# Low-part score matmuls over 64 or over 128 rows in a hybrid attention kernel

## Chip, cores and metric

The kernel runs on one NeuronCore of a Trainium2 chip, as one launch. The metric is the device time of that launch in microseconds (us), the median of the runs; a profile of one execution (its span, its instructions and their waits) stands beside it.

## What is computed

Two layers of a diffusion backbone over 512 latent tokens and 256 context tokens, model width 1024, in f32. Each layer is feed-forward (SwiGLU), token mixing, feed-forward, with modulated norms around. Layer 0 mixes with differential attention (4 heads of 2 components of width 64) and multi-head latent attention (MLA, 4 heads, width 128 without position and 64 with a rotary key that all heads share). Layer 1 mixes with a state-space scan and a neighbourhood attention (NA, 8 heads of width 64). The change touches the scores alone:

```
def diff_attend(q, k, v, lam):
    s = jnp.einsum('bqhcd,bkhcd->bhcqk', q, k).astype(jnp.float32) * (DIFF_HD ** -0.5)
    p = jax.nn.softmax(s, axis=-1)
    a = (p[:, :, 0] - lam * p[:, :, 1]).astype(v.dtype)
    return jnp.einsum('bhqk,bkhe->bqhe', a, v)
...
    k = jnp.concatenate([k_nope, k_rope], axis=-1)
...
        s_lat = jnp.einsum('bqhd,bjqmhd->bhqjm', q_r, k_win).astype(jnp.float32) * scale + bias
        s_ctx = jnp.einsum('bqhd,bkhd->bhqk', q_r, k_ctx).astype(jnp.float32) * scale
```

## The kernel before

TensorE multiplies in fp32r, a rounded form of f32. To keep precision, operands are split into a high part H (the rounded value) and a low part L (the rest), and a product is three matmuls: H·H, H·L and L·H (`mm3`, lines 211 to 215). The low parts come from ACT (a cast) and DVE (a subtraction).

Heads of width 64 fill only half of the 128 rows over which TensorE contracts. `stacked` (line 249) uses that. It makes two tiles S[0] and S[1] of 128 rows, one for each of the two heads or components in a 128-row projection. Of a query, S[e] has H in the head's own half and L in the other half; of a key, H in both halves. The other half is filled by a DMA that POOL issues (line 257). One matmul of a query's S with a key's S over 128 rows is thus H·H + L·H. What is left is the query's H with the key's L: the key's low parts of both heads lie in one tile L, a head in each half, and the second matmul runs over the 64 rows of its head. `score2` (line 260) issues both, chunk by chunk of keys, with a slice r of 64 rows in the second:

```
            for e, out in outs:
                mm(out[:, c0:c0 + n], q[0][e][:, qs], k[0][e][:, ks], start=True, stop=False)
            for e, out in outs:
                r = slice(64 * e, 64 * e + 64)
                mm(out[:, c0:c0 + n], q[0][e][r, qs], k[1][r, ks], start=False, stop=True)
```

Lines 265 and 268 are the two. A unit of differential attention (`diff`, line 1073: a head and 128 queries) calls `score2` once per component, each time for one component alone, with key chunks of 512 and 256 columns (the last two units of a head, for context queries, have the 256 alone). A unit of NA (`na_unit`, line 1668) calls it for both heads at once, with two chunks of 256. A unit of MLA (`mla`, line 1112) has for each chunk three matmuls without position (lines 213 to 215), the rotary one over 128 rows (1128), and the rotary key's low part over the 64 rows of the head's half (1129). The shared rotary key is projected into both halves, so its H and L tiles have 128 rows already.

After the scores DVE takes the maximum (line 984), ACT the exponential (987), DVE the reciprocal of the sum (989); TensorE transposes the probabilities (994) and multiplies by the values (1067). `pipeline` (line 297) steps several units in turn and fills in quanta of projections that later heads need (`pf`; in NA the output projection `po`), as much per step as `set_share` allows. The order on each engine is drawn up when the program is built.

Most tiles in SBUF come from one pool `u` of 41 buffers (`NU`). PSUM has two wide score buffers (`ps`), each for one set of scores, so that the next set can be written while the last is read.

Of the kernel before, what the change touches and what calls it, by code (L numbers as in the profile page):

```python
# [9 lines left out]
F32 = mybir.dt.float32  # L10
F32R = mybir.dt.float32r
# [65 lines left out]
class Hybrid:  # L77
# [49 lines left out]
    def wload(self, src):  # L127
# [4 lines left out]
        r = self.wraws.pop(0) if self.wraws else self.wraw(src)  # L132
        H, L = [t[:, :n] for t in self.whl()]
        nc.scalar.copy(H, r)  # L134
        nc.vector.tensor_tensor(L, r, H.bitcast(F32), ALU.subtract)  # L135
        return [(H, L)]

    def wpair(self, srcs):
        def load():
# [3 lines left out]
            for i, src in enumerate(srcs):  # L143
                nc.sync.dma_start(r[:, i * n:(i + 1) * n], src)
            H, L = [t[:, :m * n] for t in self.whl()]
            nc.scalar.copy(H, r[:, :m * n])
            nc.vector.tensor_tensor(L, r[:, :m * n], H.bitcast(F32), ALU.subtract)
            return [(H[:, i * n:(i + 1) * n], L[:, i * n:(i + 1) * n]) for i in range(m)]
        return load
# [97 lines left out]
        (nc.gpsimd if pool else nc.vector).tensor_tensor(L, src, H.bitcast(F32), ALU.subtract)  # L247

    def stacked(self, f, n, key, name):
        nc = self.nc  # L250
        S = [self.u(n, F32R, name + "S") for _ in range(2)]
        L = self.u(n, F32R, name + "L")
        for e in range(2):
            r, o = slice(64 * e, 64 * e + 64), slice(64 - 64 * e, 128 - 64 * e)
            nc.scalar.copy(S[e][r], f[r])
            nc.vector.tensor_tensor(L[r], f[r], S[e][r].bitcast(F32), ALU.subtract)
            nc.gpsimd.dma_start(S[e][o], (S[e] if key else L)[r])
        return S, L

    def score2(self, outs, q, k, qs, chunks):  # L260
        mm = self.nc.tensor.matmul
        for c0, ks in chunks:
            n = ks.stop - ks.start
            for e, out in outs:
                mm(out[:, c0:c0 + n], q[0][e][:, qs], k[0][e][:, ks], start=True, stop=False)  # L265
            for e, out in outs:
                r = slice(64 * e, 64 * e + 64)
                mm(out[:, c0:c0 + n], q[0][e][r, qs], k[1][r, ks], start=False, stop=True)  # L268

    def evac_split(self, src, H, L, scale=None):  # L270
        nc = self.nc
# [736 lines left out]
    def mixer_ab(self):  # L1008
        nc, a = self.nc, self.a
# [37 lines left out]
        def to_cat(o, gcol, idx):  # L1047
            H, L = self.u(T, F32R, "catH"), self.u(T, F32R, "catL")
            for (_, c0, n) in STREAMS:
                pt = self.pb("pt")  # L1050
                self.transposes(o[:, c0:c0 + n], n // P, pt)
                self.evac_split(pt[:, :n], H[:, c0:c0 + n], L[:, c0:c0 + n], gcol)
            cat[idx] = (H, L)

        def turned(p, n):
            at = self.u(n * P, name="at")
            for t0 in range(0, n, 4):
                m = min(4, n - t0)
                pt = self.pb("pt")
                self.transposes(p[:, t0 * P:], m, pt)  # L1060
                nc.scalar.copy(at[:, t0 * P:(t0 + m) * P], pt[:, :m * P])
            return at

        def pv(at, kts, v, hd):
            po = self.pb("po")
            for i, kt in enumerate(kts):
                nc.tensor.matmul(po[:, :P], at[:, i * P:(i + 1) * P], v[hd][:, kt],
                                 start=i == 0, stop=i == len(kts) - 1)
            return po[:, :P]
# [42 lines left out]
        def mla(hd, qt):  # L1112
            self.tick(self.rate)
            if qt == 0:
                ods[4 + hd] = self.u(T, name="om")
            o = ods[4 + hd]
            rows = slice(64 * (hd % 2), 64 * (hd % 2) + 64)
            qn, kn, qr, kr = lat["qn"][hd], lat["kn"][hd], lat["qr"][hd // 2], lat["kr"]
            kts = range(6) if qt < 4 else range(4, 6)
            n = len(kts)  # L1120
            off = kts[0] * P
            qs = slice(qt * P, (qt + 1) * P)
            sc = self.ps("sc")
            for (c0, w) in self.key_chunks(qt):
                out = sc[:, c0 - off:c0 - off + w]
                self.mm3(out, (qn[0][:, qs], qn[1][:, qs]), (kn[0][:, c0:c0 + w], kn[1][:, c0:c0 + w]), True, False)
                qe = qr[0][hd % 2]
                nc.tensor.matmul(out, qe[:, qs], kr[0][:, c0:c0 + w], start=False, stop=False)
                nc.tensor.matmul(out, qe[rows, qs], kr[1][rows, c0:c0 + w], start=False, stop=True)
            p, r, _ = self.softmax_parts(sc, n * P)  # L1130
            yield
            at = turned(p, n)
            yield
            po = pv(at, kts, lat["v"], hd)
            nc.vector.tensor_scalar(o[:, qs], po, r, None, ALU.mult)
            if qt == 5:
                yield
                to_cat(o, None, 4 + hd)
# [34 lines left out]
        for hd in range(4):  # L1173
            items.append(lambda hd=hd: self.fill_until(lambda: len(lat.get("kn", ())) > hd))
            for qt in range(6):
                items.append(mla(hd, qt))
# [783 lines left out]
```

## Time and profile before

| | |
|---|---|
| time, median of 3 runs | 2925.66 us (2924.67 to 2929.27) |
| the profiled execution: its time / its span | 2928.09 us / 2926.0 us |
| mean granted clock of TensorE | 0.988 |
| PE (matmul) busy | 2854.9 us, 98%, 16429 instructions |
| PEld (weight load) busy | 2620.2 us, 90% |
| DVE busy | 2118.0 us, 72% |
| ACT busy | 1179.9 us, 40% |
| POOL busy | 92.5 us, 3% |

PE is TensorE's matmul, PEld its weight load, which overlaps it. A matmul's record lasts from its start until its result is out, and matmuls are pipelined: how long one holds the engine is read from its start to the next one's start. In a row of the order of time, "128*128 128x512" is the array's rows and columns in use, then the operand's partitions and columns, and "x2" merges equal neighbours. In names, S is a stacked tile, L a low part, H a high part; `sc` are scores of layer 0, `nsc` of NA. A stretch's row gives each engine's busy time and count, then the granted clock and the DMA share.

### The profile page before, as it was taken

The numbers are of one execution on the slowest core, as the hardware profiler recorded it, in microseconds if no ns is written. First come the engines' busy times: TensorE is split into PE (matmuls) and PEld (weight loads), VectorE is DVE, ScalarE is ACT, GpSimd is POOL, SyncE is SP. The second block draws the span as 40 slices with busy tenths as digits, with TensorE's granted clock in tenths as the row PEclk, the third lists the DMA queues.
The fourth block names the chain that finished last, engine by engine and source line by source line (L and its number), as shares of the span: only waits on it lengthen the run. The fifth ranks groups of instructions, "written<-read, shape, count | busy, mean of one in ns | idle before, by whom it ended". The sixth has DMA issues, their size and how long they took to land. (4 is left out here: it accounts for less than half of the span.)

```text
span 2926.0 us, 41798 instructions
## 1 busy us (share of the span) xinstructions
PE 2854.9 (98%) x16429; PEld 2620.2 (90%) x16429; DVE 2118.0 (72%) x3708; ACT 1179.9 (40%) x2177; POOL 92.5 (3%) x133
## 2 busy tenths in 40 slices
PE   6999999999999999999999999999999999999998
PEld 4899999987778899999999999999889887788887
DVE  5988888787664698888879677866877967733324
ACT  4332233445554343323346332333565655432222
POOL 0000000000000000000000000000000000010100
PEclk8999999999999999999999999999999999999999
DMA  6433343242100233333323233322233334232231
GB/s 229 130 129 116 123 133 112 73 124 56 35 25 10 80 96 113 112 122 129 110 78 101 74 129 123 130 65 67 73 90 107 99 114 121 89 101 95 93 98 61
DMA packets 105989, 290.00 MB, mean 99 GB/s; under 512 B 12480, under 2 KB 25664, under 8 KB 105792
## 3 DMA queue, kind: packets, MB, share of 16 engines
q1 hardware_dynamic: 100896, 278.65, 29.6%
q0 software_dynamic: 2880, 6.56, 1.1%
q8 instruction: 129, 2.11, 0.3%
q10 hardware_dynamic: 2016, 2.12, 0.2%
q14 instruction: 68, 0.56, 0.1%
HBM read 274.89 MB, written 5.83 MB: 96 GB/s over the span
## 5 line engine op out<-in xcount | busy, mean ns | idle before, releaser
L214 PE MATMUL po<-gL,wH 128*128 128x384 f32 (+2 forms) x1271 | 431.5, 340 | 0.0
L215 PE MATMUL po<-gH,wL 128*128 128x384 f32 (+2 forms) x1271 | 428.0, 340 | 0.0
L213 PE MATMUL po<-gH,wH 128*128 128x384 f32 (+2 forms) x1271 | 424.6, 342 | 2.7 <-DVE x L684 1.4
L134 ACT CAST wH<-wraw 128x1024 fp32r<-128x1024 f32 (+2 forms) x173 | 163.9, 949 | 419.3 <-PE po L214 148.5
L748 PE MATMUL pgu<-N,wH 128*128 128x384 f32 x960 | 321.5, 340 | 3.0 <-ACT wH L155 1.6
L749 PE MATMUL pgu<-N,wH 128*128 128x384 f32 x960 | 324.2, 338 | 0.0
L750 PE MATMUL pgu<-N,wL 128*128 128x384 f32 x960 | 322.7, 337 | 0.4 <-DVE wL L156 0.4
L155 ACT CAST wH<-wraw 128x1024 fp32r<-128x1024 f32 x180 | 162.9, 908 | 394.5 <-issue 130.7
L684 DVE SCALAR_TENSOR_TENSOR x<-po,half,x 128x128 f32<-128x128 f32 (+3 forms) x459 | 208.7, 492 | 118.5 <-PE po L215 117.2
L135 DVE TENSOR_TENSOR wL<-wraw,wH 128x1024 fp32r<-128x1024 f32 (+2 forms) x173 | 190.5, 1102 | 125.3 <-ACT wH L134 119.9
L213 PEld LDWEIGHTS po<-gH,wH 128*128 128x128 f32 x1271 | 237.4, 188 | 13.2 <-DVE x L684 2.3
L214 PEld LDWEIGHTS po<-gL,wH 128*128 128x128 f32 x1271 | 239.0, 188 | 7.6
L748 PE MATMUL pgu<-b,wH 128*128 128x384 f32 x720 | 245.3, 341 | 0.3 <-DVE vz L775 0.2
L215 PEld LDWEIGHTS po<-gH,wL 128*128 128x128 f32 x1271 | 238.7, 188 | 6.8
L749 PE MATMUL pgu<-b,wH 128*128 128x384 f32 x720 | 243.1, 338 | 0.0
L750 PE MATMUL pgu<-b,wL 128*128 128x384 f32 x720 | 242.8, 337 | 0.0
L156 DVE TENSOR_TENSOR wL<-wraw,wH 128x1024 fp32r<-128x1024 f32 x180 | 187.7, 1046 | 35.0 <-ACT wH L155 34.7
L748 PEld LDWEIGHTS pgu<-N,wH 128*128 128x128 f32 x960 | 180.4, 188 | 9.4 <-DVE xw L779 2.7
L750 PEld LDWEIGHTS pgu<-N,wL 128*128 128x128 f32 x960 | 180.3, 188 | 0.8 <-DVE wL L156 0.8
L749 PEld LDWEIGHTS pgu<-N,wH 128*128 128x128 f32 x960 | 180.5, 188 | 0.0
L426 DVE SCALAR_TENSOR_TENSOR wraw<-wraw,cb 128x1024 f32<-128x1024 f32 x128 | 156.1, 1220 | 6.2 <-DMA wraw<-in_wmodT 6.1
L155 ACT CAST wH<-wsum 128x1024 fp32r<-128x1024 f32 x60 | 63.1, 1052 | 235.3 <-DVE wsum L162 175.2
(389 smaller groups left out, 6398.2 us busy)
## 6 DMA issues: line engine op xcount, KB each, us to landing
wraw<-in_win SPq DMA_DIRECT2D x176, 512.0 KB, 3.3
wraw<-in_wmodT SPq DMA_DIRECT2D x128, 512.0 KB, 3.4
wraw<-in_wout SPq DMA_DIRECT2D x96, 256.0 KB, 3.1
wraw<-in_wout SPq DMA_DIRECT2D x48, 192.0 KB, 2.5
wraw<-in_wxbc SPq DMA_DIRECT2D x16, 512.0 KB, 3.6
E<-csd SPq DMA_DIRECT2D x32, 256.0 KB, 4.8
wraw<-in_wout SPq DMA_DIRECT2D x16, 448.0 KB, 3.3
wmod<-in_wmodA SPq DMA_DIRECT2D x16, 384.0 KB, 7.2
```

The costliest lines, as they stand in the source:

```text
L134: nc.scalar.copy(H, r)
L135: nc.vector.tensor_tensor(L, r, H.bitcast(F32), ALU.subtract)
L155: nc.scalar.copy(H, src)
L156: nc.vector.tensor_tensor(L, src, H.bitcast(F32), ALU.subtract)
L213: mm(out, l[0], r[0], start=start, stop=False)
L214: mm(out, l[0], r[1], start=False, stop=False)
L215: return mm(out, l[1], r[0], start=False, stop=stop)
L426: nc.vector.scalar_tensor_tensor(junk, r, 1.0, self.cb[s], ALU.mult, ALU.mult, accum_out=acc[:, s:s + 1])
L684: self.nc.vector.scalar_tensor_tensor(xs, acc.at(P, c0, n), scal[:, d, s:s + 1], xs, ALU.mult, ALU.add)
L748: mm(bank, w[0][:, c], r[0], start=start and kk == 0, stop=False, skip_group_check=True)
L749: mm(bank, w[0][:, c], r[1], start=False, stop=False, skip_group_check=True)
L750: mm(bank, w[1][:, c], r[0], start=False, stop=kk == 3, skip_group_check=True)
```

## The change

`stacked` makes, for a key, two low-part tiles instead of one. Each has one head's low part in that head's half and zeros, written by a memset on POOL, in the other. `score2` runs the second matmul over all 128 rows: the query's L, which now stands against the other half, meets zeros. Its order is by head or component: first and second product of one, then of the other. In MLA the slice of rows goes; the low part of the query now meets the rotary key's low part, a small product that was left out before.

```
     def stacked(self, f, n, key, name):
+
         nc = self.nc
         S = [self.u(n, F32R, name + "S") for _ in range(2)]
-        L = self.u(n, F32R, name + "L")
+        Ls = [self.u(n, F32R, name + "L") for _ in range(2)] if key else [self.u(n, F32R, name + "L")] * 2
         for e in range(2):
             r, o = slice(64 * e, 64 * e + 64), slice(64 - 64 * e, 128 - 64 * e)
+            L = Ls[e]
+            if key:
+                nc.gpsimd.memset(L[o].bitcast(F32), 0.0)
             nc.scalar.copy(S[e][r], f[r])
             nc.vector.tensor_tensor(L[r], f[r], S[e][r].bitcast(F32), ALU.subtract)
             nc.gpsimd.dma_start(S[e][o], (S[e] if key else L)[r])
-        return S, L
+        return S, Ls
...
             for e, out in outs:
-                mm(out[:, c0:c0 + n], q[0][e][:, qs], k[0][e][:, ks], start=True, stop=False)
-            for e, out in outs:
-                r = slice(64 * e, 64 * e + 64)
-                mm(out[:, c0:c0 + n], q[0][e][r, qs], k[1][r, ks], start=False, stop=True)
+                for part in range(2):
+                    mm(out[:, c0:c0 + n], q[0][e][:, qs], k[part][e][:, ks], start=part == 0, stop=part == 1)
...
-            rows = slice(64 * (hd % 2), 64 * (hd % 2) + 64)
...
-                nc.tensor.matmul(out, qe[rows, qs], kr[1][rows, c0:c0 + w], start=False, stop=True)
+                nc.tensor.matmul(out, qe[:, qs], kr[1][:, c0:c0 + w], start=False, stop=True)
```

On TensorE, the first unit of head 2 in differential attention. In these rows a name's number tells one tile from another, and the size is that of the output. Before:

```order
L265 MATMUL sc_6767<-kS_6330,qS_6128 128x512
L268 MATMUL sc_6767<-kL_6332,qS_6128 128x512
L265 MATMUL sc_6767<-kS_6330,qS_6128 128x256
L268 MATMUL sc_6767<-kL_6332,qS_6128 128x256
L265 MATMUL sc_6779<-kS_6331,qS_6129 128x512
L268 MATMUL sc_6779<-kL_6332,qS_6129 128x512
L265 MATMUL sc_6779<-kS_6331,qS_6129 128x256
L268 MATMUL sc_6779<-kL_6332,qS_6129 128x256
```

and now:

```order
L270 MATMUL sc_6779<-kS_6336,qS_6134 128x512
L270 MATMUL sc_6779<-kL_6338,qS_6134 128x512
L270 MATMUL sc_6779<-kS_6336,qS_6134 128x256
L270 MATMUL sc_6779<-kL_6338,qS_6134 128x256
L270 MATMUL sc_6791<-kS_6337,qS_6135 128x512
L270 MATMUL sc_6791<-kL_6339,qS_6135 128x512
L270 MATMUL sc_6791<-kS_6337,qS_6135 128x256
L270 MATMUL sc_6791<-kL_6339,qS_6135 128x256
```

The place of each matmul is the same; the low parts of the two components are two tiles (kL_6338, kL_6339) where they were one.

On TensorE, the first unit of the second head pair in NA. Before:

```order
L265 MATMUL nsc_22875<-nS_22759,nS_22655 128x256
L265 MATMUL nsc_22875<-nS_22760,nS_22656 128x256
L268 MATMUL nsc_22875<-nL_22761,nS_22655 128x256
L268 MATMUL nsc_22875<-nL_22761,nS_22656 128x256
L265 MATMUL nsc_22875<-nS_22759,nS_22655 128x256
```

and now:

```order
L270 MATMUL nsc_22893<-nS_22774,nS_22670 128x256
L270 MATMUL nsc_22893<-nL_22776,nS_22670 128x256
L270 MATMUL nsc_22893<-nS_22775,nS_22671 128x256
L270 MATMUL nsc_22893<-nL_22777,nS_22671 128x256
L270 MATMUL nsc_22893<-nS_22774,nS_22670 128x256
```

The two low-part matmuls of a chunk, one per head, stood next to each other; now each follows its own head's first product.

On POOL, the stacking of head 2 (first the query's tiles, then the key's) and what follows it. Before:

```order
L257 DMA qS_6128<-qL_6130 64x768
L257 DMA qS_6129<-qL_6130 64x768
L257 DMA kS_6330<-kS_6330 64x768
L257 DMA kS_6331<-kS_6331 64x768
L1104 TENSOR_TENSOR r_6535<-v_6533,neghalf_91 128x6
```

and now:

```order
L261 DMA qS_6134<-qL_6136 64x768
L261 DMA qS_6135<-qL_6136 64x768
L258 MEMSET kL_6338 64x768
L258 MEMSET kL_6339 64x768
L261 DMA kS_6336<-kS_6336 64x768
L261 DMA kS_6337<-kS_6337 64x768
L1106 TENSOR_TENSOR r_6544<-v_6542,neghalf_91 128x6
```

Both memsets stand ahead of the two DMAs that fill the key's other halves.

## Rows read from the trace of the kernel before

**Rows 1.** Busy time by stretch: us from the start, length, engines, clock, DMA share, GB/s.

```profile
655.00:750.00 95.00, 94.91 (x502) 71.31 (x501) 74.31 (x151) 51.46 (x128) 5.64 (x10) 1.00 0.22 62
750.00:845.00 95.00, 91.41 (x509) 71.99 (x509) 64.95 (x141) 50.80 (x132) 7.66 (x6) 0.98 0.08 22
805.00:815.00 10.00, 8.52 (x44) 6.58 (x44) 6.24 (x12) 4.26 (x9) 1.63 (x1) 0.86 0.09 28
845.00:938.00 93.00, 93.00 (x598) 74.74 (x597) 43.81 (x98) 44.90 (x113) 2.43 (x3) 1.00 0.04 11
2400.00:2520.00 120.00, 115.58 (x801) 88.01 (x800) 91.57 (x166) 65.26 (x158) 7.59 (x13) 0.97 0.38 107
```

**Rows 2.** Lines 268 and 1129: count, duration in ns (min/median/max), first and last start, forms.

```profile
L268 PE MATMUL sc<-kL,qS x80: 379/384/626, 656.4 to 836.0; 64*128 64x256 f32 x48, 64*128 64x512 f32 x32
L268 PE MATMUL nsc<-nL,nS x64: 378/381/385, 2399.3 to 2509.4; 64*128 64x256 f32 x64
L1129 PE MATMUL sc<-krL,qrS x40: 378/385/500, 845.5 to 934.9; 64*128 64x256 f32 x24, 64*128 64x512 f32 x16
```

**Rows 3.** Order of time on PE, a component in diff: start us, us, instruction.

```profile
739.57 0.50 PE L265 MATMUL sc<-kS,qS 128*128 128x512 f32 x1
740.00 0.49 PE L268 MATMUL sc<-kL,qS 64*128 64x512 f32 x1
740.42 0.38 PE L265 MATMUL sc<-kS,qS 128*128 128x256 f32 x1
740.73 0.38 PE L268 MATMUL sc<-kL,qS 64*128 64x256 f32 x1
741.04 0.50 PE L213 MATMUL pf<-hH,wH 128*128 128x512 f32 x1
741.38 0.39 PE L214 MATMUL pf<-hL,wH 128*128 128x512 f32 x1
741.61 0.39 PE L215 MATMUL pf<-hH,wL 128*128 128x512 f32 x1
```

**Rows 4.** Order of time on PE, the end of a unit's scores in MLA.

```profile
895.03 0.28 PE L215 MATMUL sc<-knH,qnL 128*128 128x256 f32 x1
895.15 0.28 PE L1128 MATMUL sc<-krH,qrS 128*128 128x256 f32 x1
895.35 0.38 PE L1129 MATMUL sc<-krL,qrS 64*128 64x256 f32 x1
895.67 0.33 PE L994 MATMUL pt<-cst,p 128*128 128x128 f32 x1
```

**Rows 5.** Order of time on PE, a unit's scores in NA.

```profile
2434.38 0.40 PE L265 MATMUL nsc<-nS 128*128 128x256 f32 x2
2434.72 0.39 PE L268 MATMUL nsc<-nL,nS 64*128 64x256 f32 x2
2435.03 0.50 PE L265 MATMUL nsc<-nS 128*128 128x256 f32 x2
2435.47 0.38 PE L268 MATMUL nsc<-nL,nS 64*128 64x256 f32 x2
2435.78 0.44 PE L994 MATMUL npt<-cst,np 128*128 128x128 f32 x2
```

**Rows 6.** Line 365, a memset on POOL: count, ns, start, form.

```profile
L365 POOL MEMSET sc<- x1: 311/311/311, 0.8 to 0.8; 128x256 f32 x1
```

**Rows 7.** Line 257, POOL's issues of the key copies in layer 0.

```profile
L257 POOL DMA_DIRECT2D kS<-kS x8: 509/509/517, 620.5 to 736.8; - x8
```

**Rows 8.** Waits of PE, 2400 to 2520 us: us in total, times, longest.

```profile
PE nsc L265 <- DMA nS<-nS: 1.8, 3, 0.9
```

**Rows 9.** Waits of DVE for ACT, 655 to 750 us.

```profile
DVE wL L135 <- ACT wH L134: 1.8, 3, 0.9
DVE rsum L989 <- ACT p L987: 1.6, 3, 1.0
```

**Rows 10.** Waits of DVE for the exponential, 750 to 845 us.

```profile
DVE rsum L989 <- ACT p L987: 4.9, 5, 2.1
```

## Prediction

> **What bounds the kernel now.** I read the views in this order. First the stretches [rows 1], to see who is full where the change acts. The reader is to see that TensorE (PE) is busy throughout 655 to 938 us, the two attentions of the first mixer (diff to about 845, MLA after it), and 115.58 of 120 us in the neighbourhood attention (NA), at a granted clock of 1.00 or little less, which is its 2.4 GHz level. DVE is the next engine, with 74.31 of 95 us in the first half of diff, less later. So what changes PE's queue in these stretches changes the end. Then the counts [rows 2]: every low-part matmul of a score runs on 64 rows of the array, and there are 80 in diff, 40 in MLA, 64 in NA, all between matmuls over 128 rows. A duration there says little, since matmuls overlap: 379 to 385 ns at half the rows is no shorter than its neighbours. So third the order of time, where the distance from one start to the next is what a matmul holds PE [rows 3 to 5].
>
> **What a half-row matmul costs.** Undisturbed, 512 columns over 128 rows hold PE for 0.23 us (741.38 to 741.61 [rows 3]), 256 columns for 0.12 (895.03 to 895.15 [rows 4]). Around a half-row matmul three distances are longer. The full-row matmul before it: 895.15 to 895.35 is 0.20 instead of 0.12, so 0.08 on entry. The half-row one: 895.35 to 895.67 is 0.32 instead of 0.12, 740.00 to 740.42 is 0.42 instead of 0.23, so 0.20. And the first full-row matmul after it: 741.04 to 741.38 is 0.34 instead of 0.23, so 0.11.
> Diff: from 740.00 to 741.38 [rows 3] stand four matmuls (512, 256, 256, 512 columns), 1.38 us; undisturbed they would hold 0.23 + 0.12 + 0.12 + 0.23 = 0.70. That is 0.68 for two half-row matmuls with one entry among them; with the other entry 0.76, 0.38 each. Times 80: **30.4 us**.
> MLA: the 16 on 512 columns are followed by a score matmul as in diff, 16 x 0.38 = 6.1. The 24 on 256 columns close a unit, mostly with transposes behind: 895.15 to 895.67 is 0.52 for two that would hold 0.24, 0.28 each (what the first transpose pays is left out), 6.7. Together **12.8 us**.
> NA: the two heads' low-part matmuls use different halves of the rows, and there the row shows two in the time of one: "x2" spans 0.39 us [rows 5]. The unit from 2434.38 to 2435.78 takes 1.40 for eight matmuls of 256 columns; over full rows 8 x 0.12 = 0.96. So 0.44 per unit, times 16 units **7.0 us**, with the lost overlap already in it.
> Sum 50.2 us. The number of matmuls is the same, the columns too; the row count is no part of what a matmul holds PE (a full-row one holds 0.23 for 512 columns).
>
> The Trainium skill speaks against the change here: its page "TensorE: Matmul & The Clock Gate", Part 3, section "The mechanism", has matmuls in distinct row groups overlap in the array, the next tile starting some 4 ns after the first. NA's pairs agree with it (0.39 us for two). By that rule alone, with nothing paid for going in and out, the sum would be a loss: 32 pairs that become two matmuls in a row.
>
> **What is added.** Per key, two memsets on POOL of 64 x 768, 16 in all. The trace has one of 128 x 256, 311 ns [rows 6]; three times the columns bound one by 0.31 and 0.93, I take 0.7 (width counts, not rows), 11 us on POOL over the kernel, which is busy 5.64 and 7.66 us in the halves of diff [rows 1]. In diff they stand in POOL's queue ahead of the copies of the key halves, so a memset that waits for its buffer holds these. The cover is long: the last of the eight key copies issues at 736.8 [rows 7], when head 2's first unit has not begun [rows 3], and head 3 is scored six units later. Heads 0 and 1 are copied during the projections. I cost them at nothing; without that cover it is 1.4 us per head. In NA the cover is short: PE already waits three times for a key copy, 1.8 us in all [rows 8]. Each of the three can grow by what the unit just before saves, 0.44, so I take off 1.3; with both memsets in the way it would be 1.4 more per head pair, 5.6, which is for the range.
> One more of the 41 shared buffers is held per key; a wait for one falls on the memset, so its bounds are nothing and the memset's cover above. The key tiles' zero half needs no DMA and no ACT or DVE time. For MLA the rotary key's low part already fills 128 rows, so nothing is added there.
>
> **What is late next.** DVE. In 655 to 750 it is busy 74.31 us and waits 3.4 for ACT (exponentials, weight parts) [rows 9], which a faster PE does not shorten: 77.7. PE has 48 of the half-row matmuls there (14 units, of which ten use both key chunks), so it needs 95 - 48 x 0.38 = 76.8. DVE is the longer by **0.9 us**. In the second half it is 64.95 + 4.9 [rows 10] = 69.9 against 95 - 32 x 0.38 = 82.8, with room. Two queues that close will catch on each other. The row for 805 to 815 shows the size of one such catch: PE busy 8.52 of 10 and clock 0.86, so 1.5 us idle and 2.8 us at the 1.2 GHz level, which costs half of that, 1.4. I take one more of these, **2.9 us** (an estimate, one episode of that row). In MLA DVE has 43.81 of 93 us, so no loss.
> Gain: 50.2 - 1.3 - 0.9 - 2.9 = 45.1 us. Against the profiled execution (span 2926.0, its own time 2928.09) that is 2880.9 and 2883.0; that execution is 2.4 us over the median of the three runs, 2925.66, from which I get **2881 us** (2880.6).
>
> **The rivals.**
> DVE takes the place of the switches: if in diff 24 of the 48 reciprocals wait their longest 1.0 us for the exponential [rows 9] with nothing to do between, DVE needs 77.7 + 69.9 + 24 = 171.6 of 190 us and diff gains 18.4 instead of 30.4 less 3.8. With MLA's 12.8 and nothing kept in NA: 31 us, 2894.5. For: DVE is at 78% of the first half. Against: only three of the reciprocals wait there now, since other DVE work lies between.
> All of it arrives: no catch anywhere, and transposes after MLA units gain too (0.05 each at most, by rounding of the rows): 52, 2873.5.
> The long distances stay, because they belong to accumulating a second product and not to the row count: then NA loses the overlap, 32 x 0.12 = 3.8 us, 2929.5. The rule of the Trainium skill's page "TensorE: Matmul & The Clock Gate" that is told above would leave it so too. Against: L214 is also a second product on the stationary tile of the matmul before it, into the same accumulation, and it holds PE for 0.23 [rows 3]; L1128 adds to the accumulation of L215 and starts 0.12 behind it [rows 4]. What differs at L268 and L1129 is the 64 rows.
> Slower: each unit of diff starves PE long enough for the clock to fall, as at 805 to 815. At the lower level PE loses half of the time spent there. It decides from 100 us of the 190 at that level, which eats the 50.2; at 120 us the loss is 60 and the time 2935.5. Against: in the first half, where DVE is fullest, the clock is 1.00 throughout, and PE's order has no fewer fill-in matmuls than now.
>
> **How the numbers follow.** Forecast (gain 37 to 55, with everything or a catch more) 0.72; DVE-bound (20 to 37) 0.2; distances stay 0.05; slower 0.03. About 0.2% (5.9 us) is what a measurement of this kernel can tell from no change. The first two cases are faster, 0.92; the third lies within, 0.05; the last 0.03. The range leaves out the last two and the thin ends: low 2870, 55 saved, the sum with 10% for rounding; high 2897, 28 saved, the DVE rival with NA's bound of 5.6 partly in it.
>
> **What would show it.** Right: the two lines of the score matmuls and the last of MLA's five all read 128*128; start to start 0.23 and 0.12 there, no 0.42; a diff component 0.70 instead of 1.4; the stretch that was 655 to 938 some 40 us shorter, NA some 6; PE's clock still 1.00; DVE's waits for score matmuls shorter, DVE at 85 to 95% of the first half of diff. POOL has 16 memsets of 0.3 to 0.9 us, and nobody waits for them. Wrong: score matmuls over 128 rows still 0.3 or 0.4 apart (the switch was not the cost); PE waiting for exponentials or for the transposes' inputs in each unit (DVE or ACT took over); PE waiting for key copies over 2 us at a time (memsets held by buffers); a granted clock under 0.95 in diff.

## The result, and the profile after

The changed kernel took a median of 2886.94 us (2885.11 to 2888.39, 4 runs), the kernel before 2927.47 (2924.67 to 2934.94, 4 runs): a ratio of 0.985, 95% interval 0.9838 to 0.9863. That is 40.5 us faster; forecast were 2881 us and a gain of 45.1. The profiled execution took 2888.18 us, its span 2886.2.

The page of the changed kernel, its span and the busy time of each engine:

```profile
span 2886.2 us, 41850 instructions
PE 2804.7 (97%) x16429; PEld 2614.9 (91%) x16429; DVE 2114.9 (73%) x3708; ACT 1179.0 (41%) x2177; POOL 105.3 (4%) x149
```

PE does the same 16429 matmuls with 50 us less of busy time; POOL has 12.8 us more. The stretches that answer to [rows 1] (start and end in us, length, busy time and count of PE, PEld, DVE, ACT and POOL, granted clock, DMA share, GB/s) are diff in two halves, MLA, and most of NA:

```profile
659.00:740.00 81.00, 79.03 (x512) 69.54 (x512) 74.92 (x154) 51.40 (x130) 9.27 (x13) 1.00 0.26 72
740.00:821.00 81.00, 75.73 (x492) 66.48 (x492) 61.89 (x136) 48.83 (x130) 8.38 (x6) 1.00 0.09 25
821.00:900.00 79.00, 78.34 (x586) 72.91 (x585) 43.09 (x96) 43.96 (x111) 2.43 (x3) 1.00 0.05 13
2362.00:2477.00 115.00, 108.87 (x805) 87.72 (x804) 91.02 (x165) 65.88 (x160) 11.95 (x19) 0.97 0.40 114
```

The first row holds about as many matmuls and DVE instructions as the first row of before, in 81 us instead of 95. DVE is now busy 92% of it (85 to 95 were forecast) and PE has gaps; in the second row PE is idle for 5.3 us. MLA runs without a gap to speak of.

The changed lines of the changed kernel (count, duration in ns as min/median/max, first and last start, forms) answer to [rows 2] and [rows 6]:

```profile
L270 PE MATMUL sc<-kL,qS x80: 277/282/402, 659.8 to 812.7; 128*128 128x256 f32 x48, 128*128 128x512 f32 x32
L1130 PE MATMUL sc<-krL,qrS x40: 276/283/399, 822.1 to 899.0; 128*128 128x256 f32 x24, 128*128 128x512 f32 x16
L258 POOL MEMSET kL<- x8: 732/735/742, 623.0 to 726.2; 64x768 f32 x8
L258 POOL MEMSET nL<- x8: 733/736/737, 2347.0 to 2443.9; 64x768 f32 x8
```

Every low-part matmul now reads 128*128, and on 256 columns its record is 0.28 us long, as a full-row one was. A memset takes 0.735 us where 0.7 was estimated. The order of time on PE, one component of diff (it answers to [rows 3]), the end of a unit's scores in MLA ([rows 4]) and the first and last of a unit's scores in NA ([rows 5]):

```profile
729.59 0.39 PE L270 MATMUL sc<-kS,qS 128*128 128x512 f32 x1
729.82 0.39 PE L270 MATMUL sc<-kL,qS 128*128 128x512 f32 x1
730.05 0.28 PE L270 MATMUL sc<-kS,qS 128*128 128x256 f32 x1
730.17 0.28 PE L270 MATMUL sc<-kL,qS 128*128 128x256 f32 x1
730.29 0.39 PE L270 MATMUL sc<-kS,qS 128*128 128x512 f32 x1
...
859.39 0.28 PE L1129 MATMUL sc<-krH,qrS 128*128 128x256 f32 x1
859.51 0.28 PE L1130 MATMUL sc<-krL,qrS 128*128 128x256 f32 x1
859.63 0.82 PE L996 MATMUL pt<-cst,p 128*128 128x128 f32 x6
...
2399.48 0.28 PE L270 MATMUL nsc<-nS 128*128 128x256 f32 x1
...
2400.43 1.04 PE L996 MATMUL npt<-cst,np 128*128 128x128 f32 x8
```

A component takes 730.29 - 729.59 = 0.70 us instead of 1.38; MLA's last two take 0.24 instead of 0.52; NA's eight 0.95 instead of 1.40. The long distances are gone in all three places, to the hundredths that were forecast.

The weight loads show what else comes with a change of the row count. These are the loads of three matmuls of [rows 3], in the kernel before:

```profile
740.00 0.18 PEld L268 LDWEIGHTS sc<-kL,qS 64*128 64x128 f32 x1 [0.24 <-issue]
741.04 0.19 PEld L213 LDWEIGHTS pf<-hH,wH 128*128 128x128 f32 x1
741.15 0.19 PEld L214 LDWEIGHTS pf<-hL,wH 128*128 128x128 f32 x1
```

L214 follows a matmul over as many rows, and its weights are loaded from 741.15, 0.23 us ahead of its start at 741.38, while L213 still runs. L268 and L213 stand behind a change, and their loads start with them, at 740.00 and 741.04. So it is in all of diff: at each of its 160 changes load and matmul start within 0.003 us of each other, while of the 807 matmuls without a change ahead 800 have their weights loaded earlier, by 0.11 us in the median. Across a change the loads are not hidden behind the matmul ahead.

What PE waits for most in diff and MLA (us in total, times, longest):

```profile
PE pvm L213 <- ACT latH L246: 2.1, 1, 2.1
PE sc L270 <- ACT p L989: 2.0, 2, 1.5
PE pf L213 <- DVE knL L276: 1.3, 1, 1.3
```

Before, the same three were 1.1, 1.5 and 0.7 us: the first and the last have grown, and a second, short wait for an exponential has come. In NA PE still waits for the key copies 1.8 us in all, in four waits instead of the three of [rows 8], and 2.1 us, where it was 1.0, for `yH`, an operand of the output projection.

**Where the time went, by stage.** For every kernel below I split three stages of its profiled execution. A length goes from the first start of the stage on PE to the first start of the next (NA's to the last start of the output projection). *Idle* is the length less PE's busy time. *Clock* is what the 1.2 GHz level cost: the stage in pieces of about 5 us, each times one less its granted clock, added up. *Full* is what is left: PE busy at its 2.4 GHz level. A matmul's record outlasts its hold on PE, so waits shorter than that stay in *full*.

| kernel | diff: length | full | idle | clock | MLA: length | NA: length |
|---|---|---|---|---|---|---|
| before | 183.23 | 177.8 | 3.7 | 1.7 | 98.26 | 139.95 |
| after | 156.48 | 149.2 | 7.2 | 0.0 | 85.36 | 135.14 |
| e8_after (the same kernel again) | 157.45 | 148.8 | 7.0 | 1.7 | 85.35 | 136.50 |
| e1_mla_only | 183.30 | 177.9 | 3.7 | 1.7 | 85.22 | 142.49 |
| e2_diff_only | 156.46 | 149.2 | 7.2 | 0.0 | 98.46 | 140.59 |
| e3_na_only | 185.27 | 176.7 | 3.4 | 5.1 | 98.28 | 134.56 |
| e4_diff_grouped | 170.55 | 166.7 | 3.9 | 0.0 | 98.27 | 138.15 |
| e5_na_apart | 181.80 | 178.0 | 3.8 | 0.0 | 98.30 | 153.61 |
| e6_memsets | 157.31 | 148.7 | 7.0 | 1.7 | 85.40 | 131.85 |
| e7_mods_in_mla | 155.74 | 147.8 | 6.2 | 1.7 | 85.13 | 137.24 |
| e9_no_mods | 153.72 | 148.1 | 5.6 | 0.0 | 85.09 | 138.24 |
| e10_mods_triple | 160.85 | 150.2 | 10.7 | 0.0 | 86.67 | 135.42 |
| e11_before_triple | 190.83 | 176.2 | 6.1 | 8.6 | 97.81 | 140.72 |
| e12_mods_behind | 155.21 | 147.8 | 5.8 | 1.7 | 90.14 | 133.08 |

From before to after diff lost 26.75 us, MLA 12.90, NA 4.81, together 44.5. The spans differ by 39.8. Of the 4.7 us between these, 3.5 are a later start: the first score of diff starts at 659.5 us in the profile of after, at 655.9 in before's. Kernels that alter nothing up to there scatter as well: it starts at 656.5 in e3_na_only, 658.0 in e5_na_apart, 658.5 in e1_mla_only, and e8_after has it at 658.1. NA scatters too, from 138.2 to 142.5 us in kernels that leave it as it was. The five such kernels have 140.4 us there on average, the eight with the changed order and 128 rows 135.3, so NA's gain is 5.1 us by this count.

### The profile page after: what moved, and what is told of

The parts are those of the page before. It is cut to its first block, busy times and chain, and to the rows that moved or that the text cites. A ratio compares the mean times of both kernels' runs of the same rounds, so it can differ in the third digit from the quotient of the medians.

```text
span 2886.2 us, 41850 instructions
## 1 busy us (share of the span) xinstructions
PE 2804.7 (97%) x16429; PEld 2614.9 (91%) x16429; DVE 2114.9 (73%) x3708; ACT 1179.0 (41%) x2177; POOL 105.3 (4%) x149
## 5 line engine op out<-in xcount | busy, mean ns | idle before, releaser
L214 PE MATMUL po<-gL,wH 128*128 128x384 f32 (+2 forms) x1271 | 430.6, 340 | 0.0
L213 PE MATMUL po<-gH,wH 128*128 128x384 f32 (+2 forms) x1271 | 424.4, 341 | 3.4 <-ACT wH L146 1.5
L213 PEld LDWEIGHTS po<-gH,wH 128*128 128x128 f32 x1271 | 236.9, 188 | 14.5 <-ACT gH L246 2.6
L214 PEld LDWEIGHTS po<-gL,wH 128*128 128x128 f32 x1271 | 238.6, 188 | 7.4
```

Source lines behind the costliest of these rows:

```text
L213: mm(out, l[0], r[0], start=start, stop=False)
L214: mm(out, l[0], r[1], start=False, stop=False)
```

## The experiments

They ran in three groups, each beside the kernel before, whose medians there were 2928.53 us (e1 to e4), 2931.01 (e5 to e8) and 2929.43 (e9 to e12).

### One part at a time

The question is whether each of the three stages gives what its own matmuls cost, or whether one pays for another. **e1_mla_only** is the kernel before with MLA's line alone:

```
-                nc.tensor.matmul(out, qe[rows, qs], kr[1][rows, c0:c0 + w], start=False, stop=True)
+                nc.tensor.matmul(out, qe[:, qs], kr[1][:, c0:c0 + w], start=False, stop=True)
```

> The kernel before with MLA's rotary low-part matmul alone (40 of them) over 128 rows; diff and NA as before. Theory (going in and out of 64 rows costs PE 0.28 to 0.38 us each time): 12.8 us faster than before, 0.9956, all of it between the last diff unit and the output projection; DVE has room there, so nothing is lost to waits. Rival (DVE or ACT takes the place of the switches): under 6 us. Rival (the distances belong to the second product): no change.

Measured: 2916.01 us against 2928.53, ratio 0.9953 (0.9941 to 0.9966), 12.5 us faster. MLA went from 98.3 to 85.2 us, the rest stood.

**e2_diff_only** makes two padded low-part tiles for diff's keys alone, and NA keeps the old order and 64 rows:

```
+        wide = key and name != "n"
+        Ls = [self.u(n, F32R, name + "L") for _ in range(2)] if wide else [self.u(n, F32R, name + "L")] * 2
...
+            if wide:
+                nc.gpsimd.memset(L[o].bitcast(F32), 0.0)
```

> The kernel before with diff's 80 low-part matmuls alone over 128 rows (two key tiles with zeros in layer 0); MLA and NA as before. Theory: PE needs 30.4 us less, some 4 to 7 of them are lost because DVE is full in the first half of diff: 23 to 27 us faster, 0.991 to 0.992. Rival (DVE-bound): 15 to 18 us. Rival (nothing is lost): 30 us. The three parts alone should add up to the whole change's 40.5 us if the parts don't touch each other.

Measured: 2904.32 us, ratio 0.9913 (0.99 to 0.9927), 24.2 us faster; diff 156.5 us, as in after.

**e3_na_only** is the reverse (`name == "n"`), with MLA as before.

> The kernel before with NA's 64 low-part matmuls alone over 128 rows, each behind its own head's first product; layer 0 as before. Theory: each of the 16 units' scores goes from 1.40 to 0.96 us or less, 7.0 us in PE's queue, of which waits for key copies, for exponentials and for the y operands take 1 to 3: 4 to 6 us faster, 0.998 to 0.9985. Rival (the lost overlap of the two half-row matmuls decides): 3.8 us slower.

Measured: 2923.08 us, ratio 0.9983 (0.9973 to 0.9994), 5.5 us faster. A loss from the lost overlap of NA's pairs is excluded.

The three gains add up to 42.2 us. The whole change gave 40.5 in the first comparison and 43.2 in **e8_after**, the changed kernel unaltered, run again beside other experiments:

> The changed kernel again, unaltered, as the measure for the two kernels built on it in this group, and to see whether the 3.5 us by which its first 200 us were late in its first profile come again. All theories: its ratio to the kernel before is 0.985 to 0.986. Theory (the late start belongs to that execution): in this profile the first mixer's attention starts within 1.5 us of where the kernel before has it. Rival (it belongs to the change): some 3.5 us late again.

Measured: 2887.76 us against 2931.01, ratio 0.9849 (0.9836 to 0.9863). Within the intervals, some 3 to 4 us either way, the parts are independent: no stage gives back what another gains. The other thing asked of e8_after came out between the two answers: diff starts 2.2 us later than in the profile of before, where within 1.5 was expected and 3.5 was the rival. With the scatter of the starts above, nothing shows that the late start belongs to the change.

### Is it the row count?

**e4_diff_grouped** keeps every half-row matmul of before and changes their order alone: within a component, first the full-row products of both key chunks, then the half-row ones. Going in and out happens once instead of twice.

```
-        for c0, ks in chunks:
-            n = ks.stop - ks.start
...
+        sets = [chunks] if len(outs) == 1 else [[ch] for ch in chunks]
+        for group in sets:
+            for c0, ks in group:
...
+            for c0, ks in group:
```

> The kernel before with one change of order: in a diff component with two key chunks the two full-row products come first, then the two half-row ones, so that a component goes into 64 rows once instead of twice. The instructions and their row counts are the same. Theory (the cost is per time in and out): 32 of the 80 times go away, 32 x 0.38 = 12 us less in PE's queue, 9 to 12 us faster, 0.996 to 0.997; the half-row matmul on 512 columns is followed by the one on 256 after 0.23 us. Rival (each half-row matmul is slow by itself, or each second product): no change, and the distance stays 0.42.

Measured: 2917.77 us against 2928.53, ratio 0.9958 (0.9946 to 0.9971), 10.8 us faster; diff 12.7 us shorter, 11.1 of them in *full*. So the cost is not the half-row matmul's, nor that of the second product: it is paid per change of the row count. The order of time on PE in e4_diff_grouped, two components ("x2" is 512 columns, then 256):

```profile
735.03 0.51 PE L267 MATMUL sc<-kS,qS 128*128 128x512 f32 x2
735.47 0.61 PE L272 MATMUL sc<-kL,qS 64*128 64x512 f32 x2
736.01 0.62 PE L267 MATMUL sc<-kS,qS 128*128 128x512 f32 x2
736.56 0.61 PE L272 MATMUL sc<-kL,qS 64*128 64x512 f32 x2
737.11 0.50 PE L213 MATMUL pf<-hH,wH 128*128 128x512 f32 x1
737.45 0.39 PE L214 MATMUL pf<-hL,wH 128*128 128x512 f32 x1
```

Undisturbed, 512 and 256 columns hold PE for 0.35 us. The first pair takes 0.44, 0.09 more, with a change of the row count behind it alone; the next three, full or half, 0.54 to 0.55, 0.20 more, with a change at each end; the projection after them 0.34 instead of 0.23, 0.11 more, with one ahead. So a change costs 0.09 on the matmul ahead of it and 0.11 on the one behind, in either direction, 0.20 in all, and half-row matmuls in a row pay nothing between them. Where a transpose of 128 columns stands behind the change, it pays 0.055 instead of 0.11 (in MLA of before the first transpose behind a half-row matmul holds PE for 0.165 us, others for 0.11). From 736.01 to 737.11, a component with one way in and one out, are 1.10 us: 0.70 and two changes.

**e5_na_apart** takes the kernel before and puts NA's half-row matmuls apart, each behind its own head's first product: the order of the change, without its padding.

```
             for e, out in outs:
+                r = slice(64 * e, 64 * e + 64)
                 mm(out[:, c0:c0 + n], q[0][e][:, qs], k[0][e][:, ks], start=True, stop=False)
-            for e, out in outs:
-                r = slice(64 * e, 64 * e + 64)
                 mm(out[:, c0:c0 + n], q[0][e][r, qs], k[1][r, ks], start=False, stop=True)
```

> The kernel before with one change of order in NA: each head's half-row product stands behind its own head's full-row one, as the changed kernel orders them, but still over 64 rows. Instructions and row counts are the same. Theory (a price per time in and out): PE goes into 64 rows 64 times instead of 32, and two half-row products no longer overlap. A unit's scores go from 1.40 us to about 2.1 (four times 0.23 in front and 0.32 behind): 16 x 0.7 = 11 us slower, 8 to 12 with what waits cover. Rival (only the overlap counts): 3.8 us slower. Rival (order does not matter): no change.

Measured: 2944.64 us against 2931.01, ratio 1.0042 (1.0029 to 1.0054), 13.6 us slower, above the 8 to 12 expected; NA 13.7 us longer. The lost overlap alone would be 3.8. The order of time on PE in e5_na_apart:

```profile
2397.67 0.28 PE L266 MATMUL nsc<-nS 128*128 128x256 f32 x1
2397.88 0.38 PE L267 MATMUL nsc<-nL,nS 64*128 64x256 f32 x1
2398.19 0.38 PE L266 MATMUL nsc<-nS 128*128 128x256 f32 x1
2398.51 0.38 PE L267 MATMUL nsc<-nL,nS 64*128 64x256 f32 x1
2398.82 0.38 PE L266 MATMUL nsc<-nS 128*128 128x256 f32 x1
```

Each matmul, full or half, holds PE for 0.31 to 0.32 us: 0.12, 0.11 for the change ahead and 0.09 for the one behind. The expectation had 0.55 for a pair of them, which is 0.63: it left out the 0.09 ahead of each way in. So the same order of heads is dear with 64 rows and cheap with 128.

### Does anyone wait for the memsets?

**e6_memsets** is the changed kernel with each memset three times:

```
-                nc.gpsimd.memset(L[o].bitcast(F32), 0.0)
+                for _ in range(3):
+                    nc.gpsimd.memset(L[o].bitcast(F32), 0.0)
```

> The changed kernel with every memset of a key's zero half issued three times instead of once: 32 more on POOL of 0.74 us each. Theory (they are hidden): in layer 0 nothing; in NA the two key copies behind them issue 2.9 us later where POOL had no time to spare, and PE waits for at most some of it: 0 to 4 us slower than the changed kernel, under 1 us for the first two thirds of the program. Rival (memsets hold the key copies up already now): 6 to 12 us slower, so that dropping them would be worth 3 to 6.

Measured: 2884.29 us (2881.02 to 2886.62) beside e8_after's 2887.76 (2883.57 to 2889.06). The memsets in the trace of e6_memsets:

```profile
L259 POOL MEMSET kL<- x24: 732/736/776, 621.7 to 730.1; 64x768 f32 x24
L259 POOL MEMSET nL<- x24: 731/734/763, 2344.7 to 2445.6; 64x768 f32 x24
```

Tripled, they are 48, add 23.5 us to POOL, and cost nothing that shows: diff is 157.31 us against e8_after's 157.45, NA 131.9 against 136.5. The cover is long in diff, as was argued, and was enough in NA too, where the prediction called it short. The medians differ by 3.5 us in favour of the kernel with more work, so a difference of that size between two of these kernels need not be an edit's doing.

### What took back part of diff

Diff at full clock gave 28.6 us, and idle took 3.5 of it. Two causes were named: DVE is the longer in the first half, and the queues catch once more. DVE also does sixteen long passes for modulation vectors of a later stage (`mod_block`, eight blocks of two passes over 128 x 1024, 1.22 us each), which `pipeline` spreads over the steps. In after and e8_after half of the sixteen run ahead of diff and the other eight in its first half, up to 741 us. **e9_no_mods** leaves all of them out, and with them the loads of their weights:

```
     def mod_block(self, l, j, dt, streams):
         nc = self.nc
+        if l == 0 and j == 8:
+            nc.vector.tensor_copy(self.mod[l][:, j, dt, :2], self.bmod[:, l, j, dt:dt + 1].to_broadcast([P, 2]))
+            return
```

> The changed kernel without the eight blocks of DVE background work that run beside diff (the modulation's ninth vector is its bias alone, so 16 passes of 1.2 us and their loads are left out). Theory (a full DVE took some 3 of the 4.6 us that diff's gain lacks of 30.4): the diff stretch, 157.4 us in the changed kernel, comes down to 154 to 155, the run 2 to 5 us faster than the changed kernel. Rival (the lack comes from the chain of latent projections at the end of diff, where PE waits for ACT): diff stays within 1 us of 157.4. In either case the waits at the end of diff (1.6, 2.3 and 1.5 us) stay.

**e10_mods_triple** and **e11_before_triple** add two further passes to each of them, in the changed kernel and in the kernel before:

```
+            if l == 0 and j == 8:
+                extra = self.pst.tile([P, 1024], F32, tag="st", name="extra")
+                for _ in range(2):
+                    nc.vector.scalar_tensor_tensor(extra, r, 1.0, self.cb[s], ALU.mult, ALU.mult, accum_out=acc[:, s:s + 1])
```

> The changed kernel with each DVE pass of those eight blocks made three times (32 more passes of 1.2 us, 39 us of DVE, about 30 of them beside diff; the result is the same). Theory (DVE is full in diff now): DVE would need 133 + 30 = 163 us of a stretch of 157, so PE waits: diff 8 to 15 us longer. Rival (DVE still has room): diff up to 3 us longer.

> The kernel before with the same 32 more passes. Its diff stretch is 183 us, DVE busy 135 of it, so 165 fit: theory: diff 0 to 5 us longer, and less than in the changed kernel. Rival (the two kernels have the same room on DVE): the same growth as in the changed kernel.

Measured, against 2929.43: e9_no_mods 2883.9 us (ratio 0.9843, 0.9829 to 0.9856), e10_mods_triple 2890.85 (0.9865, 0.9852 to 0.9879), e11_before_triple 2936.99 (1.0023, 1.0014 to 1.0032). The medians of the changed kernel's variants differ by no more than the scatter of the starts and of NA, so diff itself says more. The whole of diff in e8_after, e9_no_mods and e10_mods_triple, in this order:

```profile
658.10:815.60 157.50, 150.54 (x970) 132.62 (x969) 132.52 (x280) 96.95 (x248) 17.63 (x19) 0.99 0.16 47
```

```profile
657.90:811.70 153.80, 148.17 (x970) 131.52 (x969) 124.66 (x259) 96.73 (x248) 16.22 (x19) 1.00 0.13 34
```

```profile
658.30:819.20 160.90, 150.25 (x964) 131.00 (x964) 153.89 (x323) 97.84 (x247) 17.91 (x21) 1.00 0.18 54
```

Without the passes diff is 3.7 us shorter than in e8_after. Of that 1.7 is clock, which after did not lose either; against after it is 2.8, with 1.6 less idle. The passes and their loads went together here, so how much of it is the passes' alone is not shown. In the first half PE's waits shrink from 1.7 us in five kinds to one of 0.3. With the passes tripled diff is 3.4 us longer than in e8_after, all of it and more in idle (10.7 against 7.0). My theory wanted 8 to 15, as the excess of DVE's total over the length of the stretch, and missed. DVE got 21.4 us more work there, not the 30 that were reckoned with, so its total, 153.9 us, stayed below the 160.9 of the stretch and there was no excess; PE lost 3.4 us all the same, a sixth of the added work. The sum alone does not set it. The waits of PE in e10_mods_triple show where it is lost:

```profile
PE sc L270 <- ACT p L993: 3.7, 5, 1.4
PE pt L1000 <- DVE p L1098: 1.8, 2, 1.5
```

The score matmuls wait until the exponential has freed their buffer, five times instead of twice, and transposes wait for a step of DVE on their input. The longest of the latter waits, from 718.93 to 720.45 us, does stand behind two passes on DVE, from 716.42 on. The second of them and the step that PE waits for:

```profile
717.68 1.22 DVE L431 SCALAR_TENSOR_TENSOR extra<-wraw,cb 128x1024 f32<-128x1024 f32 x1
719.29 1.01 DVE L1098 SCALAR_TENSOR_TENSOR p<-p,rho 128x768 f32<-128x768 f32 x1
```

Not every wait is of this kind. That for an exponential from 725.91 to 727.15 ends behind a cast of weights on ACT (725.59 to 726.64), and the maximum that the exponential needs was long done (722.66). So a pass can cost when it stands in DVE's queue ahead of something that PE waits for; that all of the 3.4 us come in this way is not shown.

In the kernel before the tripled passes cost diff 7.6 us, more than in the changed kernel, where I had expected less. The table splits it: idle rose by 2.4 us, less than the changed kernel's 3.7, and 6.9 are clock. (*Full* is 1.6 lower, so *clock* counts somewhat more than was lost: not all of the time at the lower level costs half.) The first fall of the clock in e11_before_triple; two later ones leave 0.87 and 0.83 of 10 us each:

```profile
660.50:670.50 10.00, 9.40 (x30) 5.34 (x29) 7.49 (x12) 4.54 (x11) 1.02 (x2) 0.95 0.34 92
670.50:680.50 10.00, 10.00 (x38) 7.70 (x38) 7.56 (x16) 3.03 (x7) 0.00 (x0) 0.54 0.16 54
```

The second stretch is at the 1.2 GHz level almost throughout (0.54), though PE is busy for all of it. In the first one PE waited for 0.60 us. So the idle time goes the way of the theory, its size does not, and the runs do not tell which short wait the clock answers.

### Moving the passes

If the passes cost 2 to 3 us in diff, they might be free in MLA, where DVE is busy for little more than half of the time. **e7_mods_in_mla** stops their supply during diff:

```
-        self.rate = 0.25
+        self.rate = 0.0
...
+        items.append(lambda: setattr(self, "rate", 0.4))
```

> The changed kernel with the background work on DVE (eight blocks of the next modulation, each two passes of 1.2 us) moved from the units of diff to those of MLA, where DVE has room; all that is computed is the same. Theory (DVE being full in the first half of diff took 4 us of the gain): 2 to 4 us faster than the changed kernel. Rival (the waits there come from the order of ACT's work or from the chain of the latent projections): within 1 us.

Measured: 2881.04 us against 2931.01, ratio 0.9831 (0.9818 to 0.9844), the lowest median of all. But the passes did not go where the edit put them. Their row in the trace of e7_mods_in_mla, 655 to 900 us:

```profile
L428 DVE SCALAR_TENSOR_TENSOR junk<-wraw,cb x7: 1212/1220/1224, 727.9 to 765.0; 128x1024 f32<-128x1024 f32 x7
```

Seven of the eight blocks run at 727.9 to 766.2 us, in the middle of diff: the order on each engine, drawn up when the program is built, had pulled them ahead. Diff is 1.7 us shorter than in e8_after. Of the 6.6 us between the two profiled executions most lies in stretches that the edit does not touch (the start 0.8, the stages between MLA and NA 3.3), and the intervals of the two ratios overlap. Whether it is faster than the changed kernel stays open, the more so as e6_memsets came out 3.5 us lower than e8_after with work added.

**e12_mods_behind** forces them behind MLA's first unit with an ordering dependence:

```
+            if self.mmark is not None:
+                with self.tc.issue_after(self.mmark.ins):
+                    self.tick(0.45)
```

> The changed kernel with the eight blocks held behind the first MLA unit's maximum on DVE, so that none of them stands in diff (seven of the eight had come back into diff's end in the earlier kernel that moved them); all that is computed is the same. Theory: diff 154 to 155 us as without the blocks, MLA as before at 85.4 (DVE has 43 of 79 us there): 2 to 4 us faster than the changed kernel. Rival: the load of their weights or their order delays the output projection and gives the gain back.

Measured: 2888.22 us, ratio 0.9857 (0.9843 to 0.987), no gain. Diff is 2.2 us shorter than in e8_after, MLA 4.8 longer. The longest wait of PE in e12_mods_behind, 814 to 904 us:

```profile
PE pt L996 <- DVE knL L276: 3.1, 1, 3.1
```

and what DVE did at the end of it, in the order of time:

```profile
832.24 1.22 DVE L428 SCALAR_TENSOR_TENSOR wraw<-wraw,cb 128x1024 f32<-128x1024 f32 x1
...
833.39 1.93 DVE L260 TENSOR_TENSOR qrL<-pf,qrS 64x768 fp32r<-64x768 f32 x2
835.35 0.69 DVE L276 TENSOR_TENSOR knL<-pf,knH 128x512 fp32r<-128x512 f32 x1
```

A pass of 1.22 us stands ahead of the rotary query's and the key's low parts, which PE needs next, and 1.7 us of clock are lost on top. That pass is 1.22 of the 3.1 us at most; three others ran between 825.2 and 830.1, and DVE itself waited for POOL for 1.16 us, until 831.37, so the rest is not the one pass's. DVE's spare time in MLA was no use to passes that came at this moment.

## Why the prediction was right, point by point

**The mechanism held.** The row count was the cost, not the second product: order alone gave 11 to 13 us in diff (e4_diff_grouped), and alternating cost 13.7 in NA (e5_na_apart). The prediction read three separate prices, 0.08 on entry, 0.20 on the half-row matmul, 0.11 behind it. They are the two halves of a change, 0.09 ahead and 0.11 behind, paid once on the way in and once on the way out; for a half-row matmul that stands alone this gives 0.40 where 0.38 was taken. Why a change costs anything the prediction did not say; the weight loads above, which start only with their own matmul there, are what the trace shows of it.

**Sizes.** Diff's 80 x 0.38 = 30.4 us were 28.6 in *full*, 6% less. The price itself was right: in the trace of before, the distances next to all 160 changes, at the median of each kind of matmul and less those of undisturbed matmuls of the same columns, add up to 30.6. What is short may lie on the other side: *full* of diff runs from 147.7 to 150.2 us in kernels with the same matmuls, and which short waits it holds was not taken apart. MLA's 12.8 were 12.9, and two errors cancel in that: busy time fell by 13.6, since the first transposes, left out of the forecast, gained too, and 0.7 us of idle time came, where no loss was expected. NA's 7.0 less 1.3 were 4.8 in after and 3.5 in e8_after. PE's busy time at full clock there fell by 6.5 us from before to after (the split of the table, done for NA: full 132.1 to 125.6, idle 4.4 to 6.1, clock 3.4 in both), so 7.0 was near. What was taken off was too small and put in the wrong place: the waits for key copies, which were to grow by 1.3, stayed at 1.8 us in all, and idle rose by 1.7 in after and 4.0 in e8_after through others, the wait for `yH` first (1.0 before, 2.1 and 2.8 now), which I had not named.

**What is late next.** I took off 3.8 us in diff. Idle rose by 3.5 us while the clock gave back 1.7 in after and nothing in e8_after: net 1.8 and 3.3. The size was about right, its first part for a wrong reason: I let DVE's sum exceed PE's by 0.9 us, and e10_mods_triple shows that the sum alone does not set it. What e9_no_mods shows is that the passes with their loads cost 2.8 us against after, 1.6 of it idle time; most of the rest of the rise are the two waits at the latent projections at the end of diff, for `latH` and `knL`, 1.0 and 0.6 us longer than before, and e9_no_mods has them too. The "one more catch" came as those.

**Memsets and buffers** were costed at nothing, and tripled memsets cost nothing that shows.

**The rivals.** That all of it arrives, 52 us: the three stages gave 44.5. DVE taking the place of the switches: diff would have gained 18.4 us and gained 26.75. That the long distances stay: the rows show 0.23 and 0.12. The rule of the Trainium skill named there (its page "TensorE: Matmul & The Clock Gate", Part 3, "The mechanism") describes the pairs of NA rightly, but the overlap of 3.8 us that it would have kept is less than what going in and out costs around it. Slower by the clock: no stretch of diff in after is under 1.00.

**The total.** 2886.94 us lies in the range of 2870 to 2897, 5.9 over the forecast. The stages gave 44.5 us in after and 42.1 in e8_after, of 45.1; the rest lies in the scatter of the start and of the stages that the change does not touch. That the total for NA and the 3.8 us of diff came near is in part luck: the amounts fit, the waits behind them were mostly others.

## What to carry to other kernels

Before matmuls over half the rows are put between matmuls over all of them, count the changes of the row count: each cost 0.20 us here (0.15 ahead of a transpose), more than a whole matmul of 256 columns, so zeros over the other half, or half-row matmuls in a row, were cheaper. When PE gets faster, look for what stands in another engine's queue ahead of the next thing that PE needs, and not for the largest busy share alone: DVE had time to spare in MLA, and passes moved there still made it 4.8 us longer. Split a stage into full-speed busy time, idle time and lost clock before comparing two profiles, or scatter of the clock is taken for the edit's doing.

## What the runs showed of the hardware

A change of rows costs some 0.09 us ahead of it and 0.11 behind, whichever way it goes, and as much at 512 as at 256 columns (a half-row matmul between full ones holds PE 0.20 longer with either, [rows 3, 4]); a transpose of 128 columns behind it pays 0.055. Across the change the weights are not loaded while the matmul ahead runs (160 of 160 in diff). A half-row matmul otherwise holds PE as long as a full one. Two of them on different halves run at the same time (the pair spans 0.39 us, one record 0.38, [rows 2, 5]), and the pair still pays both changes.

The clock is not the same in two executions of one program. The same 10 us of diff in e8_after and in after, each with a wait of 1.5 us shortly ahead of it and one of 2.2 within it:

```profile
788.10:798.10 10.00, 7.76 (x37) 6.02 (x36) 8.13 (x17) 4.95 (x14) 1.59 (x1) 0.83 0.08 26
```

```profile
789.40:799.40 10.00, 7.58 (x42) 5.48 (x41) 8.77 (x20) 6.02 (x18) 1.69 (x1) 1.00 0.07 26
```

In the one PE runs at the 1.2 GHz level for a third of the stretch, in the other not at all. Over all kernels diff lost between 0 and 8.6 us in this way. What decides whether the clock falls was not tried.
